# A diffusion backbone on one core: where the low halves of the convolution's output weights are made

## The chip, the cores and the metric

The kernel runs on one core of one Trainium2 chip. The core has five engines with a queue each: TensorE (PE in the profile, with PEld for its weight loads), VectorE (DVE), ScalarE (ACT), GpSimd (POOL) and SyncE (SP, which here only issues DMAs). The metric is the device time of one execution in microseconds, the median of several runs.

## What is computed

A layer of windowed attention and a layer of a Conformer convolution module on 1024 tokens of width 1024, with a prefix of 256 context tokens, then a final normalisation. All data are float32. Cut to what matters:

```python
# layer 0
o = windowed_attention(q, k, v, kc, vc, sink)
y = (o * silu(z)) @ attn_w_out            # 2048 x 1024
x = x + gate * y
# layer 1
a, gl, z = split(h @ conv_w_in + b_in, 3)
u = depthwise_conv(a * sigmoid(gl))       # 31 taps
u = silu(layernorm(u, ln_g, ln_b))
y = (u * silu(z)) @ conv_w_out            # 2048 x 1024
x = x + gate * y
return rmsnorm(x, final_g)
```

## The kernel before

**High and low halves.** The matmuls take a rounded 32-bit type (`F32R`). To keep float32's precision, each operand is split into a high half, its rounded value, and a low half, the rest, and a product is three matmuls: high by high, high by low, low by high. So every weight goes through two instructions before PE can use it: a rounding Copy on ACT (`act(hi, w, AF.Copy)`) and a subtraction `w - hi` on DVE or POOL (`split_lo`).

**Stages.** The kernel runs through a start, attention (about 105 to 845 us of the profiled span), the attention's output projection (`proj_attn`, with `Wo`), the convolution's input projection with the depthwise convolution on DVE, ACT and POOL beside it, and the last stage, the convolution's output projection (`proj_out`, with `Wp`), which begins at about 1563 us. The layer norm over channels runs in two halves of the tokens: the first beside the end of the input projection, the second (`layer_norm(1)`) inside the last stage, driven by `ln_run` from `bgB`. Its gates (`LN_AT`, `LN1_AT`) fix at which step of PE's program its mean, its sum of squares and its spread over the partitions come.

**Order.** A planner (`TileContext` with a simulated timeline) lays out the queues of ACT, DVE, POOL and SP from the program's text and its own costs. PE is kept in the order of the text (`pin("P")`). Each queue then runs strictly in its planned order, and an instruction that waits for a semaphore holds up all behind it.

**Attention.** The loop over `steps` goes through 16 heads `h` and 8 query blocks `qb`. A step issues the scores of the next block, filler matmuls of later projections (`fill`), the transposes of this block's probabilities into PSUM (`pss`), which ACT copies out as `pthi` and DVE as `ptlo`, and now and then the product with V. POOL scales the probabilities `p` once a step.

**Low parts made early.** `low_parts` (line 629) is a generator that makes low halves of output weights as filler work in attention and keeps them in DRAM. An item is one tile of 256 rows by 512 columns, 512 KB: load it (`low`), on each of its two halves a rounding Copy into `lhi` on ACT and a subtraction on POOL, then a store into `wolA` (for `Wo`) or `wolC` (for `Wp`). There are 16 items for each matrix: two column halves `m` by `NK` = 8 row pairs `kk`. Each `next(lows)` runs it to its next `yield`: load; first half; second half and store. So an item takes three steps. Line 1124 decides in which steps it advances: always while an item is open, otherwise in all heads from 1 on, but in heads with `h % 4 == 3` only in their first `LOWS` = 5 steps. A subtraction on POOL is also ordered behind the last softmax scaling (`after(..., anchor_p)`).

**The last stage.** `seqB` lists 32 steps: four passes `s` (a half of the tokens `h` by a half of the columns `m`) of 8 row pairs `kk`. A step is 24 matmuls: four blocks of tokens, two rows of the pair, three products each; `wh` and `wl` are the high and low halves of the weights, `gst` those of the activations (tile `gs`). Each tile of weights is used in two passes and loaded twice. `ahead` keeps the loads `EA` = 2 steps and the splits one step ahead in the text. `w_load` (line 1501) loads the weights' tile (`wo`) and its low half from `wolC` (`wol`); `w_split` (line 1509) makes the high half (`woh`) on ACT. At the end of a pass `evac1` takes the four accumulators from PSUM on DVE, adds the residual on DVE or POOL, squares on ACT. The second half of the layer norm ends in products with the gate `z` (`zsl`, loaded from DRAM), ten of its sixteen tiles on POOL.

**Pages.** All the big tiles are pages of one pool of 45, taken from a list of free pages in order (`pg.alloc`) and given back with `pg.free`.

Of the kernel before, what the change touches and what calls it, by code (L numbers as in the profile page):

```python
# [9 lines left out]
F32 = mybir.dt.float32  # L10
F32R = mybir.dt.float32r
# [3 lines left out]
P = 128  # L15
# [29 lines left out]
JSPLIT = 15  # L45
ZFROM = 8
EA = 2
LOWS = 5
LATE_FROM = 7
LN_AT = (1, 6, 7)  # L50
LN1_AT = ((0, 2), (1, 0), (1, 1))
# [43 lines left out]
def backbone_kernel(  # L95
# [8 lines left out]
    V, A, G, PE, SY = (InOrder(tc, e) for e in (nc.vector, nc.scalar, nc.gpsimd, nc.tensor, nc.sync))  # L104
# [8 lines left out]
    dr = ctx_stack.enter_context(tc.tile_pool(name="dr", bufs=1, space=bass.MemoryType.DRAM))  # L113
    pg = Pages(pgpool, 45, "page", 1024)
# [34 lines left out]
    def act(out, in_, func, **kw):  # L149
        return A.activation(out=out, in_=in_, func=func, **kw)  # L150

    def tt(eng, out, a, b, op):
        return eng.tensor_tensor(out=out, in0=a, in1=b, op=op)
# [4 lines left out]
    def split_lo(eng, lo, full, hi):  # L158
        return tt(eng, lo, full, hi.bitcast(F32), ALU.subtract)
# [417 lines left out]
    def after(ins, anchor=anchor):  # L577
        if anchor:
            tc.add_manual_dep(ins.ins, anchor[0].ins.name, mybir.DependencyInfo(
                mybir.DependencyClass.NoSync, mybir.DependencyReason.DATA), reason="behind the softmax")  # L580
# [39 lines left out]
    Wo = attn_w_out[0]  # L620
    Wp = conv_w_out[0]
    NK = NJ // 2
    wolA, wolC = (dr.tile([2, NK, P, 2, 512], F32, tag=n, name=n) for n in ("wolA", "wolC"))

    def pair_rows(ap, m, kk):

        return ap[kk * 256:kk * 256 + 256, m * 512:m * 512 + 512].rearrange("(a p) n -> p a n", p=P)

    def low_parts():

        items = [(pair_rows(w, m, kk), d[m, kk]) for w, d in ((Wo, wolA), (Wp, wolC)) for m in range(2) for kk in range(NK)]
        for src, dst in items:
            raw = pg.alloc(F32, [2, 512], "low")
            SY.dma_start(out=raw, in_=src)
            yield "open"
            for b in range(2):
                hi = hp.alloc(F32R, None, "lhi")
                act(hi[:, 0:512], raw[:, b], AF.Copy)
                after(split_lo(G, raw[:, b], raw[:, b], hi[:, 0:512]), anchor_p)
                hp.free(hi)  # L640
                if b == 0:
                    yield "open"
            SY.dma_start(out=dst, in_=raw)
            pg.free(raw)
            yield "shut"
# [163 lines left out]
    def early_proj():  # L809
        pg.free(*Hh, *Hl, cos, sin)  # L810
        for v in projA:
            if v == "early":
                break
            yield
# [106 lines left out]
    def job(key):  # L921
        kind, n = key
        i = cidx[key]
        wc = wsA.need(i)
        d = target(kind, n)
        wsA.load()
        late = None
        hold = [] if kind == "k" else None
        for half in PARTS[kind]:
            o = ps_g()  # L930
            gh = gemm_ctx(wc, o) if half == 2 else gemm_half(wc, half, o)
            for m, _ in enumerate(gh):
                yield
                if m == DEFER - 1 and late:
                    late()
            if half == PARTS[kind][0] and wsA.ns <= i + 1:
                wsA.split()
                wsA.load()
            late = finish(kind, n, half, o, d, hold=hold)
        if late:  # L940
            vlate[n] = late
        wsA.done(i)
        if key == ("v", NG - 1):
            for t in Hc:
                pg.free(*t)

    def run(gen):
        for _ in gen:
            pass
# [4 lines left out]
    def fill(n, until=None):  # L954
        while n > 0 and fillq and until not in finished:
            try:
                next(fillq[0][1])
                n -= 1
            except StopIteration:
                finished.add(fillq.popleft()[0])  # L960

    def enqueue(key):
        fillq.append((key, job(key)))
# [3 lines left out]
    def scores(h, qb):  # L967
        g = h // 4
        q = qt[h]
        kk = kvt[g]  # L970
        c = kk[2]
        k0, k1 = max(qb - 1, 0), min(qb + 1, TB - 1)
        nw = (k1 - k0 + 1) * P
        s = ps_s()
        w0 = 512 - nw
        qsl = slice(qb * P, qb * P + P)
        ksl = slice(k0 * P, k0 * P + nw)
        for n, (a, b) in enumerate(((0, 0), (0, 1), (1, 0))):
            PE.matmul(s[:, w0:512], q[a][:, qsl], kk[b][:, ksl], start=n == 0, stop=n == 2)
            PE.matmul(s[:, 512:768], q[a][:, qsl], c[:, b], start=n == 0, stop=n == 2)  # L980
        p = pg.alloc(F32, [1024], "p")
        sc8 = small([P, 3], name="sc", bufs=6)
        nmx, l0, ri = (sc8[:, i:i + 1] for i in range(3))
        w = nw + CT

        act(p[:, w:w + 1], nsink[:, h:h + 1], AF.Copy)
        sc = dict(scale=-SCALE, scalar=nsink[:, h:h + 1], op0=ALU.add, op1=ALU.min, accum_out=nmx)
        if qb == TB - 1:
            V.tensor_tensor_reduce(
                out=p[:, 0:w].rearrange("p (a b) -> p a b", a=2),  # L990
                in0=s[:, w0:768].rearrange("p (a b) -> p a b", a=2),
                in1=mask.rearrange("p (a b) -> p a b", a=2)[:, :, 0:256],
                **sc)
        else:
            V.tensor_tensor_reduce(out=p[:, 0:w], in0=s[:, w0:768], in1=mask[:, 640 - w:640], **sc)
        act(p[:, 0:w + 1], p[:, 0:w + 1], AF.Exp, bias=nmx, scale=-1.0, accum_out=l0)
        V.reciprocal(ri, l0)
        anchor_p[:] = [G.tensor_scalar(out=p[:, 0:w], in0=p[:, 0:w], scalar1=ri, scalar2=1.0, op0=ALU.mult, op1=ALU.mult)]
        ptile[(h, qb)] = p
# [98 lines left out]
    while len(tails) > 1:  # L1098
        tails.pop(0)()
    steps = [(h, qb) for h in range(NH) for qb in range(TB)]  # L1100
    lows = low_parts()
    lstate = ["shut"]
    pvq = deque()
# [7 lines left out]
    for i, (h, qb) in enumerate(steps):  # L1111
        if qb == 0:
            for n in (() if h % 4 == 3 else (h + 1,) if h % 4 or not h else (h, h + 1)):
                enqueue(("z", n))
                if n + 1 < NH:
                    enqueue(("q", n + 1))
        if (h, qb) == (NH - 1, EARLY_FROM - 2):
            run(lows)
        if h == NH - 1 and EARLY_FROM - 2 <= qb < EARLY_FROM:
            next(projA)  # L1120
        if (h, qb) == (NH - 1, EARLY_FROM):
            next(projA)
            fillq.append((("wo", 0), early_proj()))
        if lstate[0] == "open" or h and (h % 4 < 3 or qb < LOWS):
            lstate[0] = next(lows, "shut")
        nxt = steps[i + 1] if i + 1 < len(steps) else None
        regroup = nxt and nxt[1] == 0 and nxt[0] % 4 == 0
        if nxt and nxt[1] == 0:
            fill(1000, ("q", h + 1))
        if nxt and not regroup:  # L1130
            scores(*nxt)
        if not regroup:
            fill(15 if h and h % 4 == 0 and qb < 4 else FILL)
        if pvq:
            pv(*pvq.popleft())
        if regroup:
            g = nxt[0] // 4
            old = kvt[g - 1]
            run(job(("k", g)))
            transposes(h, qb)  # L1140
            run(job(("v", g)))
            pv(h, 1)
            pg.free(*old)
            scores(*nxt)
            vlate.pop(g)()
            continue
        transposes(h, qb)
        if qb % 4 == 3:
            pvq.append((h, qb // 4))
        for _ in range(2 if qb == 1 or qb == 6 and h % 2 else 1):  # L1150
            next(adag, None)
# [342 lines left out]
    wst, gst, x2 = {}, {}, {}  # L1494
# [6 lines left out]
    def w_load(i):  # L1501
        s, kk = seqB[i]
        m = subs[s][1]
        w, wl = pg.alloc(F32, [2, 512], "wo"), pg.alloc(F32R, [2, 512], "wol")
        SY.dma_start(out=w, in_=pair_rows(Wp, m, kk))
        SY.dma_start(out=wl.bitcast(F32), in_=wolC[m, kk])
        wst[i] = [w, wl]

    def w_split(i):
        w, wl = wst[i]  # L1510
        wh = pg.alloc(F32R, [2, 512], "woh")
        act(wh, w, AF.Copy)
        pg.free(w)
        wst[i] = (wh, wl)

# [211 lines left out]
```

## Time and profile before

| | us |
|---|---|
| median of 3 runs | 1755.38 |
| lowest and highest | 1755.21, 1758.65 |
| span of the profiled execution | 1752.9 |

The profile is one execution: a row for each instruction with its start and length, from which views are made. The views used below are the engines' busy times; the waits (who waited for whom: total us, number, longest); the groups of equal instructions (count, then busy us and mean ns, then the idle time of the engine just before them and what ended it); instructions in order of time; windows (busy us and counts of each engine in a stretch, the granted clock, the share of the DMA engines, GB/s); and the instructions of one tile (shortest, median and longest ns, first and last start). Tiles carry the program's names, `out<-in`, without their numbers. All instructions are recorded by a helper, so every row names line 89. Matmuls overlap: a row's length is longer than the distance to the next one.

### The profile page before, as it was taken

To read this page: it belongs to the slowest core of one execution; us is meant where nothing else is said; L and a number is where in the kernel's file an instruction comes from. 1 tells how busy PE (TensorE), PEld (TensorE's weight loads), DVE (VectorE), ACT (ScalarE), POOL (GpSimd) and SP (SyncE) were. 2 spreads that over 40 slices of the span, in tenths; PEclk is the share of its full clock that TensorE was granted. 3 is DMA by queue.
4 is the path that set the end of the run, shared out by engine and by line. 5 is a ranking of instruction groups with operands and counts; after the bars stand their busy time and mean duration, and the time that the engine had idled before them with its cause. 6 is when DMAs were issued, how large, how long until landed. Compare 5 with 4: busy or idle time off the path is not lost.

```text
span 1752.9 us, 23877 instructions
## 1 busy us (share of the span) xinstructions
PE 1720.7 (98%) x8420; PEld 1424.8 (81%) x8420; DVE 1148.3 (66%) x2079; ACT 889.4 (51%) x1548; POOL 895.4 (51%) x705
## 2 busy tenths in 40 slices
PE   7999999999999999999999999999999999999997
PEld 4788888888888888888888888888888888788886
DVE  6755564556546563656315189999999999867823
ACT  7555553445345444545334355554665564466731
POOL 0245654566636565653101267998898888130300
PEclk9999999999999999999999999999999999999999
DMA  9334443444334542436777733011121202377971
GB/s 313 107 82 139 136 133 85 145 147 145 100 105 143 152 142 87 136 119 203 279 250 239 241 90 105 13 54 31 43 79 36 91 30 79 120 254 243 325 264 48
DMA packets 195324, 242.45 MB, mean 138 GB/s; under 512 B 11798, under 2 KB 126790, under 8 KB 195204
## 3 DMA queue, kind: packets, MB, share of 16 engines
q1 hardware_dynamic: 188516, 230.10, 40.3%
q10 hardware_dynamic: 6688, 10.83, 2.6%
q8 instruction: 66, 1.08, 0.3%
q14 instruction: 54, 0.44, 0.1%
HBM read 188.70 MB, written 41.69 MB: 131 GB/s over the span
## 4 chain that ended last, share of the span: by engine, by line
PE 86%; DMA 5%; DVE 3%; POOL 2%; ACT 2%; issue 2%; SPq 1%; ACTq 0%; POOLq 0%; DVEq 0%
PE psg L89 44%; PE pss L89 22%; PE pso L89 19%; DMA araw_page<-in_ada_w_dram 1%; POOL rope_half L89 1%; DMA low_page<-in_conv_w_out_dram 1%; DMA rope_half<-rope_half 1%; SPq L89 1%; DMA low_page<-in_attn_w_out_dram 1%; DMA wolC<-low_page 1%; DVE mask_page L89 1%; ACT p_page L89 0%; POOL wlo_page L89 0%; POOL low_page L89 0%; DMA wraw_page<-in_attn_w_in_dram 0%
## 5 line engine op out<-in xcount | busy, mean ns | idle before, releaser
L89 POOL TENSOR_TENSOR odd_half<-odd_half,prod_half 128x513 f32<-128x513 f32 (+2 forms) x252 | 312.8, 1250 | 24.2 <-ACT prod_half L89 11.0
L89 PE MATMUL psg<-hh_page,whi_page 128*128 128x512 f32 x600 | 237.6, 396 | 0.0
L89 PE MATMUL psg<-hh_page,wlo_page 128*128 128x512 f32 x600 | 236.9, 395 | 0.0
L89 PE MATMUL psg<-hl_page,whi_page 128*128 128x512 f32 x600 | 236.8, 395 | 0.0
L89 POOL TENSOR_TENSOR wlo_page<-wraw_page,whi_page 128x1024 fp32r<-128x1024 f32 x70 | 173.1, 2475 | 104.1 <-ACT whi_page L89 83.2
L89 ACT ACTIVATE prod_half<-ubuf,dww 128x513 f32<-128x513 f32 (+2 forms) x252 | 165.1, 674 | 107.3 <-POOL odd_half L89 105.1
L89 POOL TENSOR_SCALAR p_page<-p_page,sc 128x640 f32<-128x640 f32 (+1 forms) x128 | 100.8, 787 | 224.4 <-DVE sc L89 208.7
L89 PE MATMUL psg<-h2h_page,whi_page 128*128 128x512 f32 x464 | 183.9, 396 | 0.0
L89 PE MATMUL psg<-h2h_page,wlo_page 128*128 128x512 f32 x464 | 183.0, 394 | 0.0
L89 PE MATMUL psg<-h2l_page,whi_page 128*128 128x512 f32 x464 | 182.4, 393 | 0.0
L89 DVE SCALAR_TENSOR_TENSOR pss<-ubuf,dww,pss 128x512 f32<-128x512 f32 (+3 forms) x270 | 172.3, 670 | 0.1
L89 DVE SCALAR_TENSOR_TENSOR pss<-ubuf,wsum,pss 128x512 f32<-128x512 f32 (+3 forms) x270 | 171.7, 670 | 0.2
L89 DVE TENSOR_TENSOR ptlo<-pss,pthi 128x640 fp32r<-128x640 f32 (+1 forms) x144 | 103.3, 717 | 64.0 <-ACT pthi L89 62.8
L89 ACT ACTIVATE p_page<-p_page,sc 128x641 f32<-128x641 f32 (+1 forms) x128 | 102.7, 802 | 74.1 <-DVE sc L89 69.7
L89 ACT ACTIVATE pthi<-pss 128x640 fp32r<-128x640 f32 (+1 forms) x144 | 88.6, 615 | 91.7 <-PE pss L89 86.3
L89 PEld LDWEIGHTS psg<-hh_page,wlo_page 128*128 128x128 f32 x600 | 112.9, 188 | 26.3
L89 PEld LDWEIGHTS psg<-hh_page,whi_page 128*128 128x128 f32 x600 | 113.0, 188 | 20.8 <-DVE kvc_page L89 0.2
L89 PEld LDWEIGHTS psg<-hl_page,whi_page 128*128 128x128 f32 x600 | 112.9, 188 | 20.7
L89 ACT ACTIVATE whi_page<-wraw_page 128x1024 fp32r<-128x1024 f32 x88 | 92.6, 1053 | 69.0 <-PE psg L89 25.5
L89 PE MATMUL pso<-h2l_page,whi_page 128*128 128x512 f32 x304 | 119.9, 394 | 0.0
L89 PE MATMUL pso<-h2h_page,whi_page 128*128 128x512 f32 x304 | 119.8, 394 | 0.0
L89 PE MATMUL pso<-h2h_page,wlo_page 128*128 128x512 f32 x304 | 119.6, 394 | 0.0
(244 smaller groups left out, 4105.2 us busy)
## 6 DMA issues: line engine op xcount, KB each, us to landing
wraw_page<-in_conv_w_in_dram SPq DMA_DIRECT2D x48, 512.0 KB
wraw_page<-in_attn_w_in_dram SPq DMA_DIRECT2D x40, 512.0 KB
wol_page<-wolA SPq DMA_DIRECT2D x32, 512.0 KB
wo_page<-in_attn_w_out_dram SPq DMA_DIRECT2D x32, 512.0 KB
wo_page<-in_conv_w_out_dram SPq DMA_DIRECT2D x32, 512.0 KB
wol_page<-wolC SPq DMA_DIRECT2D x32, 512.0 KB
rope_half<-rope_half ACTq DMA_DIRECT2D x80, 128.0 KB
araw_page<-in_ada_w_dram SPq DMA_DIRECT2D x32, 256.0 KB
```

The costliest lines, as they stand in the source:

```text
L89: r = f(*a, **k)
```

## The change

The items for `Wp` are taken out of `low_parts`, and `wolC` with them. In the last stage the load of the low half goes, and `w_split` makes it with two subtractions on POOL, each of 128x512, behind the Copy of the high half. For the 16 items of `Wo` that stay, a second `yield "open"` stands behind the load, so an item takes four steps, and the first Copy comes two steps behind its load. `LOWS` goes; the items advance in the heads with `h % 4` equal to 1 or 2, eight heads of eight steps for sixteen items of four steps.

```diff
-LOWS = 5
...
-    wolA, wolC = (dr.tile([2, NK, P, 2, 512], F32, tag=n, name=n) for n in ("wolA", "wolC"))
+    wolA = dr.tile([2, NK, P, 2, 512], F32, tag="wolA", name="wolA")
...
     def low_parts():
 
-        items = [(pair_rows(w, m, kk), d[m, kk]) for w, d in ((Wo, wolA), (Wp, wolC)) for m in range(2) for kk in range(NK)]
+        items = [(pair_rows(w, m, kk), d[m, kk]) for w, d in ((Wo, wolA),) for m in range(2) for kk in range(NK)]
         for src, dst in items:
             raw = pg.alloc(F32, [2, 512], "low")
             SY.dma_start(out=raw, in_=src)
+            yield "open"
             yield "open"
...
-        if lstate[0] == "open" or h and (h % 4 < 3 or qb < LOWS):
+        if lstate[0] == "open" or h % 4 in (1, 2):
             lstate[0] = next(lows, "shut")
...
     def w_load(i):
         s, kk = seqB[i]
         m = subs[s][1]
-        w, wl = pg.alloc(F32, [2, 512], "wo"), pg.alloc(F32R, [2, 512], "wol")
+        w = pg.alloc(F32, [2, 512], "wo")
         SY.dma_start(out=w, in_=pair_rows(Wp, m, kk))
-        SY.dma_start(out=wl.bitcast(F32), in_=wolC[m, kk])
-        wst[i] = [w, wl]
+        wst[i] = w
 
     def w_split(i):
-        w, wl = wst[i]
-        wh = pg.alloc(F32R, [2, 512], "woh")
+        w = wst[i]
+        wh, wl = pg.alloc(F32R, [2, 512], "woh"), pg.alloc(F32R, [2, 512], "wol")
         act(wh, w, AF.Copy)
+        for e in range(2):
+            split_lo(G, wl[:, e], w[:, e], wh[:, e])
         pg.free(w)
         wst[i] = (wh, wl)
```

## The prediction

> **What bounds the kernel now.** I read the engines' shares first.
>
> ```profile
> span 1752.9 us, 23877 instructions
> ...
> PE 1720.7 (98%) x8420; PEld 1424.8 (81%) x8420; DVE 1148.3 (66%) x2079; ACT 889.4 (51%) x1548; POOL 895.4 (51%) x705
> ```
>
> TensorE (PE) is busy for 98% of the span. Its program order is fixed, so work on ACT, DVE, POOL or the DMAs costs time only where PE waits for it. The next view is therefore the list of PE's waits, here without those of the start and of other stages.
>
> ```profile
> PE pss L89 <- DVE ptlo L89: 3.6, 2, 3.2
> ...
> PE pss L89 <- DVE sc L89: 1.3, 3, 0.9
> ...
> PE psg L89 <- DVE rope_half L89: 1.0, 1, 1.0
> ...
> PE pss L89 <- POOL p_page L89: 0.5, 1, 0.5
> ```
>
> The columns are total us, number of waits, longest. These four rows lie in attention, together 6.4 us. That is about what a change there can win, and the largest single wait is half of it. I looked at that one in the order of time, on ACT and then on PE (start, length, instruction, and in brackets the idle time ahead of it):
>
> ```profile
> 581.76 0.83 ACT L89 ACTIVATE p_page<-p_page,sc 128x641 f32<-128x641 f32 x1 [0.41 <-DVE sc L89]
> ...
> 588.64 1.15 ACT L89 ACTIVATE lhi_half<-low_page 128x512 fp32r<-128x512 f32 x2 [5.95 <-DMA low_page<-in_conv_w_out_dram]
> 589.69 0.68 ACT L89 ACTIVATE pthi<-pss 128x640 fp32r<-128x640 f32 x1
> ```
> ```profile
> 587.39 0.71 PE L89 MATMUL pss<-ident,p_page 128*128 128x128 f32 x5
> 591.29 0.44 PE L89 MATMUL pss<-kh_page,qh_page 128*128 128x384 f32 x1 [3.19 <-DVE ptlo L89]
> ```
>
> ACT runs its queue in order. From 582.7 to 588.6 its head was the rounding Copy of a low part (lhi), which waited for its load. Behind it stood the Copy pthi of the softmax's transposes; behind that DVE's ptlo; and for ptlo PE waited, because it frees the PSUM tile. So the low parts, filler work of no urgency, are what stops PE. The waits by window show two smaller cases of the same chain. First the window of 340 to 356 us, then 386 to 398, then 565 to 592:
>
> ```profile
> ACT lhi_half L89 <- DMA low_page<-in_attn_w_out_dram: 2.0, 1, 2.0
> PEld pss L89 <- DVE sc L89: 1.2, 1, 1.2
> ```
> ```profile
> ACT lhi_half L89 <- DMA low_page<-in_attn_w_out_dram: 3.4, 1, 3.4
> ...
> PEld pss L89 <- DVE ptlo L89: 0.6, 1, 0.6
> ```
> ```profile
> ACT lhi_half L89 <- DMA low_page<-in_conv_w_out_dram: 6.0, 1, 6.0
> ...
> PEld pss L89 <- DVE ptlo L89: 3.4, 1, 3.4
> ```
>
> PEld is PE's weight load, which waits first. The three stalls are 1.2 + 0.6 + 3.4 = 5.2 us. The rope's 1.0 and p_page's 0.5 have other causes.
>
> **What is removed in attention.** The groups and the issues give the prices:
>
> ```profile
> L89 POOL TENSOR_TENSOR low_page<-low_page,lhi_half 128x512 f32<-128x512 f32 x64 | 83.7, 1307 | 0.0
> ...
> L89 ACT ACTIVATE lhi_half<-low_page 128x512 fp32r<-128x512 f32 x64 | 39.6, 628 | 67.0 <-DMA low_page<-in_attn_w_out_dram 22.6 <-DMA low_page<-in_conv_w_out_dram 19.7 <-POOL low_page L89 10.2
> ```
> ```profile
> wol_page<-wolC SPq DMA_DIRECT2D x32, 512.0 KB
> ...
> low_page<-in_conv_w_out_dram SPq DMA_DIRECT2D x16, 512.0 KB
> wolC<-low_page SPq DMA_DIRECT2D x16, 512.0 KB
> ```
>
> Half of the items go: 32 of the 64 ACT Copies (20 us), 32 of the 64 POOL subtractions (42 us), 16 loads and 16 stores of 512 KB on SP. All of it lies beside PE's work, so none of it is subtracted. What counts is the waiting: 22.6 + 19.7 = 42.3 us of ACT waiting for these loads, of which PE felt 5.2.
>
> **The others a step behind.** The extra "open" puts one more softmax step between a load and its first Copy. A step's length comes from POOL's scaling of p, one a step, in a window of one head:
>
> ```profile
> 574.00:616.00 42.00, 6.45 (x8) 1.00 0.52 157
> ```
>
> That is 42 / 8 = 5.2 us a step. The longest wait for a load was 6.0 us, so 0.8 is left of it. At 586 us PE bore 6.0 - 3.4 = 2.6 us of ACT's wait without a stall, so 0.8 costs nothing. The bounds: all three stalls gone is -5.2. None gone is 0, because the planner orders ACT by the times it reckons, not by the text, and may pull the Copy forward again. All three stalls lie in heads whose number leaves 1 or 2 when divided by 4, exactly the heads that keep items (one in four steps, before one in three). New stalls I bound by as many again, +5.2, though with half the items and a longer distance nothing makes them. I take -5.2, as the distance covers the longest wait seen.
>
> **What is added in the last stage.** For each of its 32 steps two POOL subtractions of 128x512. The row of the same operation above has 1.31 us, so 2.6 us a step, 84 us in all. Here is the stage in windows (PE, PEld, DVE, ACT, POOL busy, clock, DMA share, GB/s):
>
> ```profile
> 1550.00:1600.00 50.00, 50.00 (x217) 40.30 (x216) 30.20 (x44) 27.83 (x42) 7.40 (x5) 1.00 0.71 240
> 1600.00:1650.00 50.00, 49.95 (x225) 40.67 (x224) 40.57 (x61) 35.73 (x54) 17.23 (x12) 1.00 0.91 319
> 1650.00:1700.00 50.00, 50.00 (x218) 40.61 (x217) 21.42 (x56) 23.40 (x39) 5.02 (x4) 1.00 0.86 304
> ```
>
> POOL has room: even in its fullest window 17.2 + 50 / 5.6 x 2.6 = 40 of 50 us. Whether each part is there in time depends on the lead of the rounding Copy woh, which the subtraction follows, over PE. Its times, PE's, and the number of Copies up to 1654 us:
>
> ```profile
> L89 ACT ACTIVATE woh_page<-wo_page x32: 1036/1059/1063, 1528.5 to 1703.6; 128x1024 fp32r<-128x1024 f32 x32
> ```
> ```profile
> L89 PE MATMUL pss<-woh_page,gs_page x352: 387/394/804, 1562.8 to 1743.2; 128*128 128x512 f32 x176
> ```
> ```profile
> 1500.00:1654.00 154.00, 80.59 (x255) 47.98 (x255) 18.98 (x18) 1.00 0.70 242
> 1654.00:1656.00 2.00, 1.79 (x8) 1.13 (x6) 1.06 (x1) 1.00 1.05 391
> ```
>
> PE's 32 steps take (1743.4 - 1562.8) / 32 = 5.64 us each. The first Copy leads by 34 us. The 19th lies between 1654 and 1656, while step 19 begins at 1562.8 + 18 x 5.64 = 1664.3: a lead of over 8 us, and this is about the shortest. With 1.3 for the first low half and 2.6 for both, 5 us are left. So the added work costs nothing. Its cover is this lead; without it each late step would cost what it is late.
>
> In return 32 loads, 16.8 MB, leave the stretch where the DMA engines are at 0.71 to 0.91, and SP issues 32 fewer DMAs. ACT waited there for the weights:
>
> ```profile
> ACT woh_page L89 <- DMA wo_page<-in_conv_w_out_dram: 37.3, 13, 8.3
> ```
>
> So the lead should grow. But PE hardly waits in this stage: all that its row above shows is one matmul of 804 ns among 394, so the gain is 0 to 0.4. I take 0. The page for the low half is now taken at the split, not at the load, which holds one page less; I cost that at 0.
>
> **The sum.** -5.2 + 0 + 0 on the profiled span gives 1747.7. The runs' median of 1755.38 is 2.5 us above the profiled span, which I take to lie outside it. Forecast: 1755.4 - 5.2 = 1750.2 us, with 1747.5 (the other waits gone too, the rope's 1.0, p_page's 0.5 and some of the start) to 1752.5 (the longest of the three remaining in part) as its own range.
>
> **Rivals.** *The wait stays* (no change). The Copies that remain sit in the same heads, and the planner pulls them forward until its own reckoned landing of the load, so ACT's head still waits. For it speaks how often it waits now:
>
> ```profile
> ACT lhi_half L89 <- DMA low_page<-in_attn_w_out_dram: 22.6, 10, 3.6
> ...
> ACT lhi_half L89 <- DMA low_page<-in_conv_w_out_dram: 19.7, 9, 6.0
> ```
>
> That is 19 waits in 32 items: the Copy starts as the load lands. Against it: only half of the items are left. Half of 5.2 or less is won, 1752.8 to 1755.4; I name 1754.1.
>
> *DVE is held at the layer norm's gate.* PE's order fixes where it transposes the reciprocal deviations r, and there is no slack there:
>
> ```profile
> 1619.95 0.16 DVE L89 TENSOR_TENSOR r<-rr,rq 128x4 f32<-128x4 f32 x1
> ...
> 1620.26 1.13 PE L89 MATMUL pso<-ident,r 128*128 128x128 f32 x8
> ```
> ```profile
> L89 DVE TENSOR_TENSOR gs_page<-v_page,gs_page x40: 676/684/1789, 1546.3 to 1665.8; 128x512 fp32r<-128x512 f32 x40
> ```
>
> DVE's split of gs usually takes 0.68 us but reached 1.79, 1.1 more. If DVE is held like this two or three times in the chain that ends in r, PE waits 2.2 to 3.3: 1750.2 + 2.7 = 1752.9. The Trainium skill has a rule on this, in "SBUF — State Buffer", section "Who interferes with whom": a DVE instruction with two inputs in SBUF contends with a GpSimd instruction that reads SBUF, and the second to issue waits for the first. The 1.79 above agrees, as 0.68 plus most of a POOL operation; by the rule the chance grows with the time that POOL is busy there.
>
> *POOL comes late* (slower). POOL's queue is in order too, and in the last stage it holds the products of the second layer norm, which wait for ACT and for their own loads:
>
> ```profile
> 1625.65 6.64 POOL L89 TENSOR_TENSOR v_page<-v_page,zsl_half 128x512 f32<-128x512 f32 x5 [14.30 <-DMA wo_page<-in_conv_w_out_dram]
> ...
> 1648.81 1.29 POOL L89 TENSOR_TENSOR v_page<-v_page,zsl_half 128x512 f32<-128x512 f32 x1 [4.04 <-DMA zsl_half<-zsd]
> ```
>
> In the text of the program all sixteen channel tiles of this norm stand ahead of the split for step 12, counted from 0. If the queue keeps that order, its first half is ready at 1650.1 + 1.3 = 1651.4, but PE wants it at 1562.8 + 12 x 5.64 = 1630.5: 21 us late, so 1750.2 + 21 = 1771. If it stands behind half of them, about 10 late: 1760. It makes the kernel slower once a split is over 5.2 + 3.5 = 8.7 us late. For it: the bracketed waits, 14.3 and 4.0. Against: ACT's woh ran 8 to 34 us ahead of PE, so the planner does go by readiness there, and POOL was idle for 14.3 us before these products, room for five splits.
>
> **How the numbers follow.** A measurement of this kernel tells about 0.2% from no change, 3.5 us: faster is below 1751.9, slower above 1758.9. Chances: forecast 0.49, the wait stays 0.22, DVE held 0.08, POOL late 0.21. Of the forecast 0.46 lies below 1751.9, and 0.03 of the others: faster 0.49. The rest of the first three is no change: 0.30. Slower is POOL late: 0.21. The range is 1747.5 to 1762: it reaches into POOL's case and leaves out its upper half, 0.1, and little below.
>
> **What would show it.** Right: ACT's wait of lhi for its loads far below 42.3 us; no PE wait over 1 us on ptlo or sc in attention; POOL rows wol_page<-wo_page,woh_page x64 near 1.3 us; the DMA share of 1600 to 1700 us well below 0.86; PE without waits after 1563 us. Wrong: PE waiting for POOL's wol_page or DVE's r in the last stage, or for ptlo in heads 1, 2, 5, 6, 9, 10, 13, 14; or a new wait in a stage that the change doesn't touch, since the planner lays out every queue anew.

## The result and the profile after

| | before | after |
|---|---|---|
| median of 10 runs each, us | 1755.61 | 1762.19 |
| lowest and highest | 1753.30, 1758.65 | 1758.43, 1763.79 |
| span of the profiled execution | 1752.9 | 1758.3 |

The ratio of after to before is 1.0034, with a 95% interval of 1.0027 to 1.0042. The change makes the kernel slower, by 0.34% or about 6 us. The profiled execution of after took 1760.13 us, 1.8 more than its span. The prediction had said 5 us faster, and the time lies just outside its range. That it lies so near the upper end is no merit: the range went up to 1762 for a rival, "POOL comes late", that did not happen.

The rows below name line 88 or 89, where each kernel has the recording helper. First the page's shares:

```profile
span 1758.3 us, 23762 instructions
...
PE 1720.7 (98%) x8420; PEld 1424.1 (81%) x8420; DVE 1170.4 (67%) x2079; ACT 876.3 (50%) x1516; POOL 949.3 (54%) x737
```

PE does the same 1720.7 us of work in a span that is 5.4 us longer, so the question is where PE waits. DVE has the same 2079 instructions as before, yet 22 us more busy time: they last longer. The list of PE's waits of the changed kernel, from the top:

```profile
PE pso L88 <- DVE r L88: 7.3, 1, 7.3
...
PE pss L88 <- DVE sc L88: 1.6, 1, 1.6
...
PE pso L88 <- DVE ptlo L88: 1.3, 1, 1.3
```

The 3.2 us on ptlo has gone. At the top stands one wait of 7.3 us that was not there: for r, the reciprocal deviations of the layer norm's second half, in the last stage. PE's order of instructions is the same in both kernels, so the nth matmul of one can be set against the nth of the other. Worked out from both traces, after less before (smaller steps are left out):

```
us (before)   step    offset from here on, and the matmul there
 189          +1.5    +1.8    pso <- ptlo, waits for DVE
 354          -1.2    -0.2    pss <- kh, qh  (stall gone)
 395          -0.7    -1.1    pss <- kh, qh  (stall gone)
 591          -3.4    -5.5    pss <- kh, qh  (stall gone)
 722          -0.7    -6.2    pss <- ident, p
 764          +1.0    -5.2    pss <- ident, p, waits for POOL (in after at 758)
 824          +1.8    -3.0    pss <- ident, p, waits for DVE (in after at 821)
1620          +7.3    +4.0    pso <- ident, r, waits for DVE
1620 to 1622  +1.4    +5.4    the same matmuls at a lower clock
```

So attention gains, as forecast, but gives part of it back, and PE comes to the gate (the place in its order where it needs r) 3.3 us earlier than before. There it loses 7.3 + 1.4 us. Now DVE at that place, in order of time (start, length, instruction, count):

```profile
1608.14 1.78 DVE L88 TENSOR_TENSOR x_page<-x_page,xr_page 128x512 f32<-128x512 f32 x1
1609.84 6.92 DVE L88 TENSOR_TENSOR x_page<-x_page,fg_page 128x512 f32<-128x512 f32 x4
1616.69 1.75 DVE L88 TENSOR_TENSOR gs_page<-v_page,gs_page 128x512 fp32r<-128x512 f32 x1
1618.36 0.15 DVE L88 TENSOR_SCALAR ms<-pso 128x4 f32<-128x4 f32 x1
1618.43 2.28 DVE L88 TENSOR_TENSOR gs_page<-v_page,gs_page 128x512 fp32r<-128x512 f32 x2
1620.63 0.16 DVE L88 RECIPROCAL rr<-sq 128x4 f32<-128x4 f32 x1
1620.72 1.66 DVE L88 TENSOR_TENSOR gs_page<-v_page,gs_page 128x512 fp32r<-128x512 f32 x1
1622.30 1.21 DVE L88 TENSOR_TENSOR rq<-rr 128x4 f32<-128x4 f32 x1
...
1623.95 0.16 DVE L88 TENSOR_TENSOR r<-rr,rq 128x4 f32<-128x4 f32 x1
```

And POOL and PE in the same stretch:

```profile
1609.32 10.24 POOL L88 TENSOR_TENSOR wol_page<-wo_page,woh_page 128x512 fp32r<-128x512 f32 x6
1620.29 3.21 POOL L88 TENSOR_TENSOR wol_page<-wo_page,woh_page 128x512 fp32r<-128x512 f32 x2 [0.73 <-DMA wo_page<-in_conv_w_out_dram]
```
```profile
1624.26 2.05 PE L88 MATMUL pso<-ident,r 128*128 128x128 f32 x8 [7.32 <-DVE r L88]
```

POOL runs eight of the new subtractions nearly back to back, 10.24 / 6 = 1.71 us each. In that time DVE's instructions on 128x512 take 6.92 / 4 = 1.73 us in place of 0.68, and in the single rows each ends about half a microsecond behind a subtraction: the rows read as if the two engines took turns. Even the tiny product rr times rr, 128x4, takes 1.21 us. Those of these rows that last longer have two inputs in SBUF. Beside them stand ms from pso, 0.15 us, and the reciprocal, 0.16, with one input each, at their usual length. The tile views show it for the whole stage (shortest, median and longest ns), first before, then after:

```profile
L89 DVE TENSOR_TENSOR x_page<-x_page,fg_page x16: 677/683/1789, 1610.1 to 1745.8; 128x512 f32<-128x512 f32 x16
```
```profile
L88 DVE TENSOR_TENSOR x_page<-x_page,fg_page x16: 692/1748/1799, 1609.8 to 1751.2; 128x512 f32<-128x512 f32 x16
L88 DVE TENSOR_TENSOR x_page<-pss,gate_page x11: 673/681/692, 1602.2 to 1749.0; 128x512 f32<-128x512 f32 x11
L88 POOL TENSOR_TENSOR wol_page<-wo_page,woh_page x64: 1283/1322/2487, 1525.4 to 1721.7; 128x512 fp32r<-128x512 f32 x64
```

The product with fg, both inputs in SBUF, goes from 0.68 to 1.75 us in the median. The product with gate, one input in PSUM, stays at 0.68 throughout. Summed over the instructions from 1608.1 to 1623.5 us, DVE is held for some 9.5 us: eight of 128x512 by about 1.06 each and one of 128x4 by 1.06, the first of them beside an addition of the residual on POOL, the others beside subtractions. Taken off, that would put r at about 1614.6 in place of 1624.1, ahead of PE, which was free at 1616.9. This is the earliest it could be: before the change DVE stood idle for 3.4 us in this stretch, waiting for ACT, and with before's last stage 0.6 us of PE's wait is left (e1 below).

The last 1.4 us are a second cost of the same wait. Windows of PE (busy us, count, granted clock, DMA share, GB/s):

```profile
1616.00:1624.00 8.00, 0.94 (x5) 0.79 0.31 96
1624.00:1631.00 7.00, 6.74 (x27) 0.75 0.34 102
1631.00:1640.00 9.00, 9.00 (x41) 1.00 0.64 201
```

When PE starts again, the granted clock is down for some microseconds: the eight transposes of r take 2.05 us in place of 1.13.

### The profile page after: what moved, and what is told of

It reads as the page before. It is cut to its first block, busy times and chain, and to the rows that moved or that the text cites. A ratio compares the mean times of both kernels' runs of the same rounds, so it can differ in the third digit from the quotient of the medians.

```text
span 1758.3 us, 23762 instructions
## 1 busy us (share of the span) xinstructions
PE 1720.7 (98%) x8420; PEld 1424.1 (81%) x8420; DVE 1170.4 (67%) x2079; ACT 876.3 (50%) x1516; POOL 949.3 (54%) x737
## 4 chain that ended last, share of the span: by engine, by line
PE 90%; DMA 4%; DVE 3%; issue 1%; ACT 1%; POOL 1%; SPq 1%; ACTq 0%; DVEq 0%; POOLq 0%
PE psg L88 47%; PE pss L88 22%; PE pso L88 20%; DMA araw_page<-in_ada_w_dram 1%; SPq L88 1%; DVE x_page L88 1%; DMA rope_half<-rope_half 1%; DMA x_page<-in_x_dram 0%; DMA wo_page<-in_conv_w_out_dram 0%; DMA wraw_page<-in_attn_w_in_dram 0%; DMA ozf_page<-ozd 0%; DVE gs_page L88 0%; POOL rope_half L88 0%; POOL wlo_page L88 0%; DVE hf_page L88 0%
## 5 line engine op out<-in xcount | busy, mean ns | idle before, releaser
L88 POOL TENSOR_TENSOR wol_page<-wo_page,woh_page 128x512 fp32r<-128x512 f32 x64 | 95.0, 1513 | 54.4 <-ACT woh_page L88 42.4
```

Of the source, the lines that this page charges most:

```text
L88: r = f(*a, **k)
```

## The experiments

The theory after this reading: the attention part gains, the last part loses at the gate, and it loses because POOL's reads of SBUF hold DVE's instructions with two inputs there. Rivals: the planner's new order of DVE at the gate (two gs splits stand in the chain to r that stood elsewhere before); POOL's load as such; the position of the gate.

**Each part alone.** First the changed attention with a last stage that loads its low halves (those of the other matrix, from `wolA`: the same traffic and work, other values); then the changed last stage with all 32 items still made in attention.

```diff
 e1, against after
-        for e in range(2):
-            split_lo(G, wl[:, e], w[:, e], wh[:, e])
+        SY.dma_start(out=wl.bitcast(F32), in_=wolA[m, kk])   # in w_load
 e2, against after (the condition for a step and wolC also as in before)
-        items = [... for w, d in ((Wo, wolA),) ...]
+        items = [... for w, d in ((Wo, wolA), (Wp, wolC)) ...]
...
-            yield "open"
```

> Only the attention half of the change: low_parts as changed, but in the last stage a low half is loaded from DRAM as before (from wolA, so low halves of the other matrix are multiplied; the traffic and the work are those of before), and POOL makes none there. Theory (the stall at the layer norm's gate costs the change its gain, attention wins): the trace of the changed kernel is 3.3 us ahead of before when PE reaches the gate, so 1755.6 - 3.3 = 1752.3 us, with PE's wait for r under 0.5 us. Rival (the attention part is itself the loss, or wins nothing): 1755.6 or above.

Measured: 1752.77 us (1751.27 to 1754.89; ratio to before 0.9981, 0.9972 to 0.9989).

> Only the last-stage half: attention as before with all 32 items (those of Wp are still made and stored, but nobody loads them), POOL makes the low halves in the last stage. Theory: PE waits some 7 us for r and runs some 7 us at half clock behind it, 8.8 us in all, and nothing is won in attention: 1755.6 + 8.8 = 1764.4 us. Rival (the loss comes from the changed attention, by another order of pages or queues): 1755 to 1757.

Measured: 1766.14 us (1765.18 to 1767.58; ratio 1.0059, 1.0047 to 1.0071). The longest wait of PE in e2:

```profile
PE pso L89 <- DVE r L89: 7.5, 1, 7.5
```

The parts are separate, and they nearly add up: -3.5 and +9.9 us against the 1756.24 of before in these runs. In e1 the wait for r is 0.6 us; in e2 it is 7.5, with before's attention. The loss belongs to the last stage alone.

**The gate two steps later.** If only the chain at this gate is late, moving PE's demand for r by two steps of 5.5 us should hide it.

```diff
-LN1_AT = ((0, 2), (1, 0), (1, 1))
+LN1_AT = ((0, 2), (1, 0), (1, 3))
```

> The changed kernel with the layer norm's last gate two steps (11 us) later in PE's program, so that r has 11 us more. Theory: PE's wait for r, 7.3 us, and the half clock behind it go: 1762.2 - 8.8 = 1753.4 us, if the second half of the norm is still in time for the third pass. Rival (PE would lose the same time to POOL's late low halves or elsewhere in the stage): 1760 or above.

Measured: 1762.53 us (1761.94 to 1766.46; ratio 1.0044, 1.0032 to 1.0056), a miss by 9 us. The wait for r went, and others came, the longest of 5.0 us. PE's longest wait in e3, and DVE in windows (busy us, count, clock, DMA share, GB/s):

```profile
PE pss L88 <- DVE gs_page L88: 5.0, 1, 5.0
```
```profile
1610.00:1616.00 6.00, 6.00 (x6) 1.00 0.49 154
...
1660.00:1670.00 10.00, 9.97 (x12) 1.00 0.34 107
1670.00:1680.00 10.00, 9.83 (x10) 1.00 0.18 52
1680.00:1690.00 10.00, 9.79 (x32) 0.59 0.54 140
```

All that follows the gate on DVE, the sixteen tiles of the norm's second half and their gs splits, comes later too, and runs into the next stretch of subtractions, where DVE is full for 30 us. On this reading what is lost is DVE's time, not one place in its order. Not all of the miss is the stage's: the profile is of the longest of e3's six executions, and in it PE reached the stage 0.3 us behind before, where after was 3.3 ahead.

**POOL as busy, but reading little.** Each subtraction of 128x512 is replaced by one of 128x8 and three memsets over the same tile, so that POOL writes as long but hardly reads. The low halves are then zero beyond the first 8 columns.

```diff
-            split_lo(G, wl[:, e], w[:, e], wh[:, e])
+            split_lo(G, wl[:, e, 0:8], w[:, e, 0:8], wh[:, e, 0:8])
+            for n in (512, 512, 200):
+                G.memset(wl[:, e, 0:n].bitcast(F32), 0.0)
```

> The changed kernel, but each POOL subtraction of 128x512 is replaced by one of 128x8 and three memsets of 512, 512 and 200 columns over the same tile, so that POOL is about as busy there but hardly reads SBUF (the low halves are zero, so that product is left out in value). The order on DVE at the gate keeps the same sixteen instructions ahead of the gate's arithmetic, within two places. Theory (DVE's instructions with two inputs in SBUF are held by POOL's reads): x*fg and gs fall from 1.75 back to 0.69 us beside POOL, PE's wait for r is under 1 us, 1753.4 us. Rival (the planner's order on DVE, with two more gs splits ahead of r, or POOL's load as such): the wait for r stays near 7 us, 1762.

Measured: 1751.97 us (1749.52 to 1754.04; ratio 0.9978, 0.9969 to 0.9987). Here is POOL in the stretch before the gate, first in after, then in e4 (busy us and count, clock, DMA share, GB/s), and then the product with fg in e4:

```profile
1600.00:1624.00 24.00, 21.85 (x14) 0.93 0.50 160
```
```profile
1600.00:1624.00 24.00, 21.74 (x51) 1.00 0.60 186
```
```profile
L88 DVE TENSOR_TENSOR x_page<-x_page,fg_page x16: 668/693/1836, 1606.5 to 1742.9; 128x512 f32<-128x512 f32 x16
```

POOL is busy for the same 21.8 us, and DVE runs at 0.69 us; PE's wait for r is 0.6. So POOL's load and the time at which it works are not what costs, and neither is DVE's order: four gs splits stand in the chain to r here too. The Trainium skill says this in "SBUF — State Buffer", section "Who interferes with whom": a DVE instruction with two inputs in SBUF contends with a GpSimd instruction that reads SBUF, not with one that only writes it, and one with at most one SBUF input does not contend, outside the modes in which DVE takes both of its port pairs, which `tensor_scalar` can enter. The traces agree: 1.75 us beside subtractions, 0.69 beside memsets, 0.68 for the product with gate from PSUM. The exception matters too. One-input TENSOR_SCALARs were held, first in e4 beside memsets (usually 0.16 us), then in e3 beside subtractions (usually 0.47):

```profile
1615.49 1.63 DVE L88 TENSOR_SCALAR rq<-rq 128x4 f32<-128x4 f32 x1
```
```profile
1678.43 1.46 DVE L88 TENSOR_SCALAR x_page<-x_page,r 128x512 f32<-128x512 f32 x1
```

The first stands in the chain to r, and its 1.5 us is more than the 0.6 that PE still waited in e4. That the mode is the reason is not shown: no run changes it.

**One read in place of two.** A copy of the weights reads one tile; the low halves are then the weights themselves.

```diff
-            split_lo(G, wl[:, e], w[:, e], wh[:, e])
+            G.tensor_copy(out=wl[:, e], in_=w[:, e])
```

> The changed kernel with each of POOL's 64 subtractions replaced by a copy of the weights to the same page, an instruction that reads one tile of SBUF in place of two; the low halves are then the weights themselves. Theory (a read of POOL holds DVE's second input, whether POOL reads one tile or two): x times fg_page stays well above 0.68 us wherever it meets a copy, PE waits for r, and the time is 1757 to 1762 us, by how long a copy lasts. Rival (it takes two inputs on both sides): x times fg_page at 0.69 us, no wait for r, 1752 us.

Measured: 1750.29 us (1749.63 to 1753.52; ratio 0.9971, 0.9962 to 0.9981). The time is the rival's, but the rows are not. The copies, then the stretch on POOL and on DVE:

```profile
L88 POOL CAST wol_page<-wo_page x64: 609/616/1181, 1523.0 to 1700.7; 128x512 fp32r<-128x512 f32 x64
```
```profile
1608.18 4.12 POOL L88 CAST wol_page<-wo_page 128x512 fp32r<-128x512 f32 x4
```
```profile
1608.70 2.11 DVE L88 TENSOR_TENSOR x_page<-x_page,fg_page 128x512 f32<-128x512 f32 x2
1610.74 0.15 DVE L88 TENSOR_SCALAR ms<-pso 128x4 f32<-128x4 f32 x1
1610.81 1.02 DVE L88 TENSOR_TENSOR gs_page<-v_page,gs_page 128x512 fp32r<-128x512 f32 x1
```

DVE is held by a copy too, to 2.11 / 2 = 1.06 us. A single read on POOL is enough. But a copy is half as long (0.62 against 1.32 us), so it holds for 0.37 us in place of 1.06, and POOL is soon done; PE does not wait. So the price goes with how long POOL reads, as far as these two lengths show.

**The subtractions on DVE.**

```diff
-            split_lo(G, wl[:, e], w[:, e], wh[:, e])
+            split_lo(V, wl[:, e], w[:, e], wh[:, e])
```

> The changed kernel with the 64 subtractions of the last stage on DVE in place of POOL. Theory (on POOL each of them holds DVE's instructions with two inputs in SBUF to 1.75 us; on DVE each costs its own 0.68 us and holds nothing): x times fg_page and the gs splits go back to 0.68 us. From the first gate's opening at 1585 to r lie six and a half steps with two subtractions each, 9 us of DVE, against some 6 us in which DVE had nothing to do there in the kernel without subtractions: r about 3 us late in place of 7.3, the time 1756 to 1758 us. Rival (DVE takes them up in its idle time): 1752.5 us. Rival (any 64 instructions more on the two engines cost as much): 1762 us.

Measured: 1763.54 us (1762.78 to 1765.06; ratio 1.0048, 1.0034 to 1.0061), a miss by some 6 us. The product with fg is no longer held, but an earlier link of the chain is late: qa, the copy of the sum of squares, which DVE builds up from sixteen tiles.

```profile
PE pso L88 <- ACT qa_half L88: 6.3, 1, 6.3
```
```profile
L88 DVE TENSOR_TENSOR x_page<-x_page,fg_page x16: 677/680/695, 1618.0 to 1755.7; 128x512 f32<-128x512 f32 x16
```

I had counted DVE's idle time over the whole stretch up to r. The sum of squares must be done several microseconds sooner, and its additions stood between the subtractions. DVE has no room ahead of this gate, whether it is filled or held. The time is that of the rival "any 64 instructions more cost as much", but as a rule that rival fails: in n3 64 instructions more on POOL, and in e4 four times as many, cost nothing at the gate that PE felt beyond 0.6 us.

**Ten of the 32 steps without subtraction.** Those whose subtractions fell on the two stretches in which DVE was full load a tile from DRAM (the other projection's, of the same size); the other 22 keep theirs on POOL.

```diff
+CLEAR = (10, 11, 12, 13, 14, 19, 20, 21, 22, 23)
...
+        if i in CLEAR:
+            wl = pg.alloc(F32R, [2, 512], "wol")
+            SY.dma_start(out=wl.bitcast(F32), in_=wolA[m, kk])
```

> The changed kernel, except that ten of the 32 steps (10 to 14 and 19 to 23, whose subtractions fell on the two stretches in which DVE was full, 1600 to 1623.5 us and 1660 to 1680.6 us) load a low part from DRAM (the other projection's, as data of the same size) and have no subtraction; the other 22 steps keep theirs on POOL. Theory (it decides only what POOL does while the gate's chain runs on DVE): no wait for r, 1752 to 1754 us. Rival (44 subtractions hold DVE's instructions elsewhere and it comes late all the same, as it did when the gate was opened later): 1757 us or more.

Measured: 1752.72 us (1749.38 to 1757.13; ratio 0.9982, 0.9971 to 0.9993), as the theory said: PE's wait for r is 0.7 us, and no other is listed in the stage. The 44 remaining subtractions cost nothing that can be seen; it is the twenty beside a full DVE that cost.

**The spacing alone, for all 32 items.** The part that pays, without the one that loses. To keep three steps an item, both halves are split in one step.

```diff
 against before
             yield "open"
+            yield "open"
             for b in range(2):
...
-                if b == 0:
-                    yield "open"
```

> The kernel before with one edit in attention: between an item's load and its split lies a second step of attention, and both halves are split in one step, so that an item still takes three steps and all 32 items are made there; the last stage is before's, with its 64 loads and no subtraction on POOL. Theory (attention's stalls come from a Copy that waits at ACT's head for its load, and the last stage's loss from POOL's subtractions): the stalls at 354, 547 and 591 us go and nothing is lost at the gate, so 1755.6 - 3.5 = 1752.1 us. Rival (attention gains because it has 16 items fewer, not because of the spacing): 1755.6 us. Rival (two Copies in one step hold ACT and with it the exponentials): 1757 us or more.

Measured: 1749.39 us (1747.31 to 1750.46; ratio 0.9964, 0.9950 to 0.9978), the lowest median of all, and 2.7 us better than the theory's 1752.1. PE is 5.8 us ahead of before from 591 us on and keeps that to the end, and ACT's waits of lhi for the loads fall from 42.3 to 16.6 us, the longest from 6.0 to 4.2. So the 32 items do not stand in the way. That the distance between load and Copy is what gains fits these rows and those of after, which has the distance with two split steps; but n1 also puts both Copies in one step, and no run has that without the distance.

**Why attention gave some back.** n1 had none of the new waits at 189, 758 and 824 us. To see whether splitting an item over two steps makes them, e1 with both halves in one step:

```diff
 against e1
-                if b == 0:
-                    yield "open"
```

> The kernel of e1_attention_part (attention as in the changed kernel with 16 items, the last stage loading its low parts) with one line out: both halves of an item are split in one step, as in n1_spaced_all, so that an item takes three steps in place of four. What it is to tell: PE stood 5.8 us ahead of the kernel before at the last stage in n1 and only 1.8 to 3.0 us in the kernels with the changed attention, which had gained the same three stalls and then waited anew at 189, 758 and 824 us. Theory (a second step with the split of the other half is what brings the new waits): they go, and the time is that of n1, 1749 to 1750 us. Rival (they come from where the 16 items lie, heads 1 and 2 of each four): they stay, 1752 to 1753 us.

Measured: 1754.52 us (1749.05 to 1756.35; ratio 0.9982, 0.9970 to 0.9993), no better than e1. The waits at those three places did go, but the profiled execution has a new one, at 415 us:

```profile
PE pss L88 <- POOL p_page L88: 2.9, 1, 2.9
```
```profile
412.23 1.30 POOL L88 TENSOR_TENSOR rope_half<-rope_half,sin_page 128x512 f32<-128x512 f32 x1 [4.28 <-DMA rope_half<-rope_half]
413.61 1.29 POOL L88 TENSOR_TENSOR rope_half<-rope_half,rope_half 128x512 f32<-128x512 f32 x1
415.64 1.26 POOL L88 TENSOR_TENSOR ql_page<-rope_half,qh_page 128x512 fp32r<-128x512 f32 x1 [0.74 <-ACT qh_page L88]
416.88 0.80 POOL L88 TENSOR_SCALAR p_page<-p_page,sc 128x640 f32<-128x640 f32 x1
```

POOL waits here for a transfer of the rope, does its three products, and only then scales the probabilities that PE wants. This isn't an instruction of the low parts at all. Neither theory holds as it was put. As far as these single traces go, each layout of the queues has small collisions of its own, of 1 to 3 us, in places that the edit does not touch. The runs of n5 differ by 7 us from lowest to highest, so how much of that wait each has is open.

## Why the prediction was wrong, step by step

**The stalls in attention: right.** Three were to go, 5.2 us; at 354, 395 and 591 us PE gains 1.2 + 0.7 + 3.4 = 5.3. The mechanism is confirmed by ACT's waits for the loads, 42.3 us in all before, now one row:

```profile
ACT lhi_half L88 <- DMA low_page<-in_attn_w_out_dram: 5.4, 3, 2.8
```

With half of the items left, half of the waiting would have been 21 us. With it falls the rival "the wait stays".

**"Nothing makes new stalls" in attention: wrong by 4.3 us.** PE lost 1.5, 1.0 and 1.8 us anew; smaller gains elsewhere in attention, some 2 us, made up for part of that. The prediction named a new wait in an untouched stage only among what would prove it wrong, and put no price on it. At 758 us POOL has p right behind a weight split of 2.42 us.

```profile
754.94 2.42 POOL L88 TENSOR_TENSOR wlo_page<-wraw_page,whi_page 128x1024 fp32r<-128x1024 f32 x1
757.34 0.97 POOL L88 TENSOR_SCALAR p_page<-p_page,sc 128x640 f32<-128x640 f32 x1
```

Before, the same split stood one place earlier, ahead of the rope's last product, and PE did not wait. The other two were not followed to their cause, and what decided that the queues came out like this was not settled. Nor is the size fixed: the same attention reached the last stage between 4.8 us ahead of before (n3) and 0.5 behind (n2), and the loss at 824 us alone went from 1.2 to 3.3 us.

**The last stage at 0: this is the step that failed.** What it argued was right. POOL had room (41.0 of 50 us in the window of 1600 to 1650, where 40 were forecast), the subtractions' shortest length is 1.28 us, PE never waits for POOL's low halves, and with that "POOL comes late" falls. But "so the added work costs nothing" looked only at those who wait for POOL's result. The cost went another way, through what POOL reads while it works: 7.3 us of PE's wait for r and 1.4 us of lower clock behind it, where the prediction had put 0.

**The rival that was right was priced too low.** "DVE is held at the layer norm's gate" named the place, the tile r, the row of 1.79 us and the rule. It counted two or three held instructions, 2.2 to 3.3 us, and gave it a chance of 0.08. There were nine, some 9.5 us, of which 7.3 reached PE. The count was there to be had. The prediction itself worked out POOL at 40 of 50 us in this window, where before it was at 17; DVE was at 40.6 of 50. DVE's chain from 1608 us to r has twelve instructions with two SBUF inputs, so at 0.8 of the time some ten of them meet POOL. The 1.79 of the gs splits was the longest, not the only one: four of the 40 took 1.77 to 1.79 us, each beside an instruction on POOL. Their small number shows how seldom POOL worked before, not how seldom the two collide.

**The idle PE's second cost, 1.4 us, was in no case.** And the 32 loads fewer, taken at 0, can't be told from 0: DMA's share in 1600 to 1650 fell from 0.91 to 0.56, while PE had not waited for them.

**The sum as measured**, on the spans: -3.3 in all up to the gate, +7.3 for r, +1.4 for the clock, makes +5.4 = 1758.3 - 1752.9. With -5.2, 0 and 0 the forecast had the three stalls right, but not what attention gave back, and it put nothing for what the last stage lost. Its step of 2.5 us from the profiled span to the median also took different executions together; within the profiled execution of after that step is 1.8.

## What to carry to other kernels

Before moving elementwise work to GpSimd, look beyond who waits for its result: multiply the share of time for which GpSimd will read SBUF by the number of VectorE instructions with two SBUF inputs on the critical chain there, and price each by what one is held (here 1.06 us beside a subtraction of 1.3 us, 0.37 beside a copy of 0.62). This is an estimate drawn from one gate of one kernel. If the chain has no slack, keep GpSimd still in just that stretch, load from DRAM what it would have made there, or have one of VectorE's inputs come from PSUM. And separate a change's parts before judging it: here the edit of n1, one more step between a load and its use with both halves in one step, is worth 0.36% by itself, and in the change the last stage's loss hid a gain of that kind.

## What the hardware showed that was not expected

The hold does not depend on DVE's size of work: 128x4, usually 0.16 us, took 1.21; 128x512, usually 0.68, took 1.75. The rows read as if each waited out the subtraction under way and then ran: the small product ended 0.02 us behind one. The subtractions in turn follow each other at 1.71 us in place of their usual 1.32, so that both lose.

The clock falls behind gaps of PE. After gaps of 7.3 us (after), 6.3 (n2) and 5.0 (e3) the granted clock went down; here n2 and e3, PE's windows behind the gap:

```profile
1620.00:1627.00 7.00, 6.44 (x19) 0.50 0.45 145
```
```profile
1686.00:1693.00 7.00, 6.96 (x18) 0.57 0.89 248
```

Shorter gaps went both ways. Around the gap of 3.2 us that before has at 588 us it stayed at 1.00:

```profile
588.00:594.00 6.00, 2.81 (x15) 1.00 0.36 125
594.00:600.00 6.00, 6.00 (x35) 1.00 0.43 137
```

But it went down behind a gap of 2.4 us in e2, at 588 us too, and behind one of 3.1 us in n2, at 820 us:

```profile
590.00:594.00 4.00, 3.44 (x11) 0.57 0.22 66
```
```profile
824.00:829.00 5.00, 4.70 (x18) 0.66 1.04 406
```

So a wait of some microseconds can cost more than itself, 1.4 us behind the 7.3 of after. The Trainium skill, "TensorE: Matmul & The Clock Gate", section "What's actually happening", gives a half-rate state after an idle window of about 3.4 us. The gaps from 5.0 us up agree with that; those of 2.4 and 3.1 us, behind which the clock went down, do not, and between 2.4 and 3.2 us these traces show no sharp limit.
